# Two PSUM banks set aside for the rows that gathered expert rows are multiplied with

## The chip, the core and the metric

The kernel runs on one core of one Trainium2 chip. The metric is the device time of one execution in microseconds. TensorE appears as PE, VectorE as DVE, ScalarE as ACT, GpSimd as POOL and SyncE as SP.

## What is computed

One layer over 128 context tokens and 512 latent tokens, five blocks of 128 rows with 1024 columns. Each block goes through a modulated norm, a projection into two head groups (retention, and attention over a neighbourhood of the grid plus the context), an output projection, and a retrieval from 16384 single-neuron experts (PEER). The part that the change touches is the retrieval:

```python
def peer(x, wq, keys, u, v):
    q = (xb @ wq).reshape(TOKEN_BLOCK, PEER_HEADS, PEER_DKEY)
    s1 = jnp.einsum('nhd,hkd->nhk', q[..., :half], keys[:, 0])
    s2 = jnp.einsum('nhd,hkd->nhk', q[..., half:], keys[:, 1])
    v1, i1 = lax.top_k(s1, PEER_TOPK)
    v2, i2 = lax.top_k(s2, PEER_TOPK)
    ...
    eidx = jnp.take_along_axis(cidx, sel, axis=-1)
    gate = jax.nn.softmax(top, axis=-1)
    act = jax.nn.gelu(jnp.einsum('nd,nhkd->nhk', xb, u[eidx]))
    return jnp.einsum('nhk,nhkd->nd', gate * act, v[eidx])
```

For each row of a block, 8 heads choose 16 experts each. Its 128 rows of `u` are multiplied with the row itself (`xb`, called x2 in the kernel), and the products weight 128 rows of `v`.

## The kernel before

Block 0 holds the context tokens, blocks 1 to 4 the latent tokens. `ctx_front` takes block 0 up to its expert scores. `lat_front` does the same for the latent blocks: common projections, then block 1 (`ROUNDS[0]`), then blocks 2 to 4 (`ROUNDS[1]`). In `mix`, `attend` runs the neighbourhood attention one unit (a head of a block) after another, and `retain` the retention. `close` does the output projection, the second norm (`modulate2`, which makes x2) and the scores (`key_scores`).

`gathers` runs beside this. For each of the five blocks it does 128 steps of kind "u": an indirect DMA from POOL's queue brings 128 rows of `u` (512 KB) into a slot of `gslots`, and one DVE instruction multiplies them with x2 and sums along the row. The slot is then free for another gather. Before each block a step of kind "x2" brings the block's x2. The top-16 searches (`topk`) are DVE work as well. At the end come 128 steps of kind "v" for block 4, which DVE sums up in PSUM.

For blocks 0 to 3 the sum over `v` is a dense product. `Dense.build` turns a block's choices and weights into a 128 x 128 x 128 table W, by one-hot matrices (two DVE comparisons with `iota2`, two ACT scalings and two small matmuls per pair of rows). `product` then streams all of `v` through PE, first for blocks 0 and 1, then for blocks 2 and 3. The builds for blocks 2 and 3 overwrite the tables of blocks 0 and 1 behind the first product. The second product needs the last build.

PSUM has eight banks of 512 columns. `bank()` takes one between two bounds, which `within` sets for a piece of work. `attend` had banks 0 to 3, and `retain`, `project` and `close` banks 4 to 7 while they ran beside it. One unit of attention takes two banks for its scores and two for its transposes, beside the bank `bo` that collects the outputs of a pair of heads.

The program is not emitted as written. Every call is recorded in `Plan`, which finds what each instruction depends on (memory cells, one cell for each bank) and orders them all by a list scheduler with costs of its own. `keep` (L365 in every row is the line that issues) hides the source lines, so rows are told apart by tiles and shapes: `psum<-arena,w 128x128` and `128x384` are key_scores with a weight tile, `128x256` with `iota` is a build, `dots` is a gather's multiply.

The places that the prediction speaks of:

```python
    gslots = [zone[1]] + zone[6:]
    ...
                b2, b = bank(), bank()
                mm(b2.ap[:, :P], lq, kctx.ap[q, p, :], True, True)
                mm(b.ap, lq, nkT.ap[q, p, :], True, True)
    ...
                nc.vector.scalar_tensor_tensor(g, g, 1.0, x2p[0], op0=OP.mult, op1=OP.mult,
                                               accum_out=dots[b % 2][:, h, k:k + 1])
```

Four more slots join `gslots` when `lat_front` has used its inputs, and one when `close` has ended; block 3's x2 goes to PSUM (banks 6 and 7) and so gives its slot back.

Of the kernel before, what the change touches and what calls it, by code (L numbers as in the profile page):

```python
# [17 lines left out]
OP = mybir.AluOpType  # L18
AX = mybir.AxisListType

D = 1024
P = 128
# [346 lines left out]
def layer(ctx: ExitStack, tc: tile.TileContext, a: dict):  # L369
# [31 lines left out]
    ar.limit = (TOT - ZONE) // UNIT  # L401
    ar.soft = 48 * 256 // UNIT
    zone = [shaped(ar.tile[:, TOT - ZONE:], [SLOTS, D])[:, i] for i in range(SLOTS)]
    gslots = [zone[1]] + zone[6:]
    ps = Mem(pp.tile([P, 8 * 512], F32, name="psum"), 8 * 512, 512)
    xres = hb.tile([5, P, D], F32, name="xres")
    xmod = hb.tile([5, P, D], F32, name="xmod")
# [5 lines left out]
    def bank():  # L413
        return ps.alloc([512], lo=banks[0], hi=banks[1])
# [498 lines left out]
    def key_scores(key, bl, x2T):  # L913
        T = P * len(bl)
        for m4 in range(4):
            bs = [bank() for _ in range(4)]
            for qt in range(4):
                w = S.get(("wq", key, m4, qt))
                for m in range(4):
                    for e in range(2):  # L920
                        c = 2 * qt + e
                        mm(bs[m].ap[:, :T], w[:, e, P * m:P * m + P], x2T[:, c, :], c == 0, c == 7)
                S.done()
            q = ar.alloc([4, T])
            for m, b in enumerate(bs):
                nc.scalar.copy(q.ap[:, m], b.ap[:, :T])
                ps.free(b)
            for i, blk in enumerate(bl):
                b = bank()
                for m in range(4):  # L930
                    mm(b.ap[:, P * m:P * m + P], q.ap[:, m, P * i:P * i + P], keysT.ap[:, 4 * m4 + m, :], True, True)
                if blk == 2:
                    t = half()
                    nc.scalar.copy(t, b.ap.rearrange("q (m k) -> q m k", m=4))
                    ps.free(b)
                    ready[blk, m4] = t
                    yield
                    continue
                t = ar.alloc([4, P], top=blk < 1)
                nc.scalar.copy(t.ap, b.ap.rearrange("q (m k) -> q m k", m=4))  # L940
                ps.free(b)
                if blk < 2:
                    ready[blk, m4] = t
                else:
                    nc.sync.dma_start(scd[blk, m4], t.ap.rearrange("q m k -> q (m k)"))
                    ar.free(t)
                    ready[blk, m4] = "dram"
                yield
            ar.free(q)


    def ctx_front():
# [114 lines left out]
        make_gates(0, ("g1", "sh2", "a2"))  # L1067
        yield from out_proj(0, 0, [oN.ap], [oR.ap], [xc.ap])
        ar.free(oR, oN)
        x2T = ar.alloc([8, P])  # L1070
        yield from modulate2(0, 0, xc.ap, zone[0], x2T.ap, 0)
        ar.free(xc)
        ar.free(*[gates.pop((n, 0)) for n in ("g1", "sh2", "a2")])
        yield from key_scores(0, [0], x2T.ap)
        ar.free(x2T)
# [9 lines left out]
    def lat_front():  # L1085
# [183 lines left out]
        def each(bl, fn, out):  # L1269
            for i in bl:  # L1270
                out[i] = yield from fn(i)
                yield
# [27 lines left out]
            yield from transposed(r, rqT)  # L1300

        def mix(bl):
            return both(within(4, 8, each(bl, retain, oR)), within(0, 4, attend(bl)))

        def close(key, bl, last):
            xs = []
# [19 lines left out]
            else:  # L1326
# [2 lines left out]

        S.quota = NRING - 2  # L1330
        yield from project(1, ROUNDS[0])
        yield from both(within(4, 8, project(2, ROUNDS[1])),
                        within(0, 4, chain(each(ROUNDS[0], retain, oR), attend(ROUNDS[0]))))
        make_gates(1, ("g1", "sh2", "a2"))
        make_gates(1, ("g2",))
        ar.free(mrow, selr, selc, scs)
        ar.free(hT, ct)
        lend(XTRA)
        yield from both(within(4, 8, close(1, ROUNDS[0], False)), mix(ROUNDS[1]))
        close_lent()  # L1340
        ar.free(nkT, kctx, vctx, Sst, *o[6].values())
        yield from close(2, ROUNDS[1], True)
# [90 lines left out]
    STEPS = 36  # L1433

    cready = {}
    x2p, x2b = [zone[0]], []

    def gathers():
        seq = []
# [36 lines left out]
        while n < len(seq):  # L1476
# [7 lines left out]
            n += 1  # L1484
            if kind == "u":
                h, k = divmod(s, 16)
                nc.vector.scalar_tensor_tensor(g, g, 1.0, x2p[0], op0=OP.mult, op1=OP.mult,
                                               accum_out=dots[b % 2][:, h, k:k + 1])
                hp, q = divmod(s, 32)
                nxt = (b, hp + 1) if hp < 3 else (b + 1, 0)  # L1490
# [17 lines left out]
                    nc.vector.tensor_mul(c, c, z1)  # L1508
                    cready[b, hp - 1] = cready[b, hp] = True
            elif kind == "x2":  # L1510
                if "lat" not in done:
                    x2p[0], g = g, x2p[0]
                else:
                    if b == 3:
                        gslots.append(x2p[0])
                        x2b.append(ps.alloc([D], lo=6))
                        x2p[0] = x2b[0].ap
                    for hf in range(2):
                        nc.scalar.copy(x2p[0][:, 512 * hf:512 * hf + 512], g[:, 512 * hf:512 * hf + 512])
            elif kind == "v":  # L1520
                h, k = divmod(s, 16)
                if s == 0:
                    ps.free(*x2b)
                    accv = ps.alloc([D], lo=6)
                    nc.vector.tensor_scalar(accv.ap, g, cw[b][:, h, k:k + 1], None, op0=OP.mult)
                else:
                    nc.vector.scalar_tensor_tensor(accv.ap, g, cw[b][:, h, k:k + 1], accv.ap, op0=OP.mult, op1=OP.add)
            elif kind == "g2":
                held = g
            else:  # L1530
                finish_with(4, [accv.ap[:, 0:512], accv.ap[:, 512:]], held, g)
                mark.append(len(nc.ops) - 7)
                done.add("v4")
# [279 lines left out]
```

## Time and profile before

| | |
|---|---|
| device time, median of 3 runs | 1914.18 us (1909.31 to 1915.98) |
| device time of the profiled execution | 1914.02 us |
| span of the profiled execution | 1912.2 us |
| PE, DVE, ACT, POOL busy | 94%, 77%, 28%, 43% of the span |
| mean granted TensorE clock | 0.947 |
| moved by DMA | 658.22 MB, mean 344 GB/s |

The span is what the trace covers; the device time is 1.8 us longer. A busy PE is not one at its peak: at a granted clock of 0.5 the same matmul takes twice as long.

### The profile page before, as it was taken

Reading aid. Unit: us, or ns where it says so; the run is one execution under the profiler, and the core shown is the slowest. Engines: PE = TensorE matmul, PEld = TensorE weight load, DVE = VectorE, ACT = ScalarE, POOL = GpSimd, SP = SyncE. Lnnn points to the kernel's source line nnn. Section 1 sums busy time; section 2 is a strip of 40 time slices with the busy share of each in tenths; the row PEclk is TensorE's granted clock in tenths of the full one; section 3 lists DMA queues with packets and bytes.
Section 4 is the critical chain, followed back from the end, with each engine's and each line's share of the span. In section 5 each row is a group of like instructions: output and inputs, shape, how many; then the busy total and the mean of one; then the engine's idle time right before and its main releaser. Section 6 shows DMA issues by size and latency. Waiting matters only on the chain.

```text
span 1912.2 us, 21190 instructions
## 1 busy us (share of the span) xinstructions
PE 1798.2 (94%) x6096; PEld 1074.3 (56%) x6096; DVE 1468.8 (77%) x3785; ACT 532.4 (28%) x1368; POOL 825.7 (43%) x779
## 2 busy tenths in 40 slices
PE   7989999999989979977999999899997999999997
PEld 2438454455955546656544444455565666666665
DVE  2245998777787799999999998778999565666666
ACT  1225321134433424699311110123574000000000
POOL 0000556543145456533555554444535444444442
PEclk9998999999968889976899999999997999999999
DMA  9997879988768799966899999999988999999998
GB/s 363 314 330 245 305 275 335 385 317 321 265 199 288 264 325 383 376 180 196 317 409 409 407 403 409 386 408 403 386 266 285 409 409 409 409 410 409 409 409 342
DMA packets 203693, 658.22 MB, mean 344 GB/s; under 512 B 22572, under 2 KB 25900, under 8 KB 203448
## 3 DMA queue, kind: packets, MB, share of 16 engines
q0 software_dynamic: 110592, 402.70, 56.7%
q1 hardware_dynamic: 92984, 254.16, 35.2%
q8 instruction: 49, 0.80, 0.2%
q14 instruction: 68, 0.56, 0.1%
HBM read 645.51 MB, written 11.27 MB: 343 GB/s over the span
## 4 chain that ended last, share of the span: by engine, by line
PE 46%; DMA 32%; DVE 16%; issue 4%; ACT 2%; POOL 0%; DVEq 0%; SPq 0%; POOLq 0%; ACTq 0%
PE psum L365 46%; DMA arena<-in_u,idx 15%; DMA arena<-in_v,idx 12%; DVE arena L365 11%; ACT arena L365 2%; DMA w<-in_w_ada 2%; DVE psum L365 1%; DMA w<-in_w_in 1%; DVE i L365 1%; DVE oh L365 1%; DVE vi L365 1%; DMA arena<-in_x 1%; DMA arena<-in_w_ada 0%; DMA arena<-in_selc 0%; DMA g2d<-arena 0%
## 5 line engine op out<-in xcount | busy, mean ns | idle before, releaser
L365 PE MATMUL psum<-w,arena 128*128 128x512 f32 (+1 forms) x2548 | 1099.5, 603 | 17.1 <-DVE arena L365 6.5
L365 POOL DMA_INDIRECT arena<-in_u,idx x640 | 702.5, 1098 | 918.0 <-DVE arena L365 482.7
L365 PEld LDWEIGHTS psum<-w,arena 128*128 128x128 f32 (+1 forms) x2548 | 561.5, 229 | 459.1 <-issue 288.6
L365 PE MATMUL psum<-arena 128*128 128x128 f32 (+5 forms) x2532 | 551.1, 370 | 57.6 <-DVE arena L365 29.4
L365 PEld LDWEIGHTS psum<-arena 128*128 128x128 f32 (+2 forms) x2532 | 378.2, 208 | 270.1 <-issue 152.5
L365 DVE SCALAR_TENSOR_TENSOR arena<-arena 128x1024 f32<-128x1024 f32 (+6 forms) x451 | 489.2, 1092 | 33.2 <-DMA arena<-in_u,idx 27.7
L365 DVE SCALAR_TENSOR_TENSOR arena<-arena,psum 128x1024 f32<-128x1024 f32 x256 | 308.6, 1215 | 88.2 <-DMA arena<-in_u,idx 87.9
L365 ACT ACTIVATE arena<-arena 128x128 f32<-128x128 bf16 (+7 forms) x626 | 237.8, 433 | 223.8 <-PE psum L365 108.0
L365 ACT COPY arena<-psum 128x512 f32<-128x512 f32 (+3 forms) x360 | 204.7, 580 | 331.9 <-PE psum L365 301.2
L365 DVE SCALAR_TENSOR_TENSOR psum<-arena,cw,psum 128x1024 f32<-128x1024 f32 x127 | 163.7, 1289 | 94.8 <-DMA arena<-in_v,idx 94.5
L365 DVE TENSOR_TENSOR arena<-iota,arena 128x256 bf16<-128x256 bf16 (+1 forms) x512 | 162.1, 355 | 32.1 <-PE psum L365 26.9
L365 POOL DMA_INDIRECT arena<-in_v,idx x128 | 120.2, 939 | 143.6 <-DVE psum L365 118.7
L365 PE MATMUL psum<-arena,w 128*128 128x128 f32 (+1 forms) x640 | 135.5, 371 | 1.4 <-ACT arena L365 1.4
L365 PEld LDWEIGHTS psum<-arena,w 128*128 128x128 f32 x640 | 95.4, 202 | 31.6 <-ACT arena L365 2.2
L365 PE MATMUL psum<-ident,arena 128*128 128x128 f32 x372 | 70.0, 317 | 27.7 <-DVE arena L365 25.0
L365 PEld LDWEIGHTS psum<-ident,arena 128*128 128x128 f32 x372 | 52.0, 165 | 65.7 <-DVE arena L365 29.0
L365 DVE TENSOR_TENSOR arena<-arena 128x256 f32<-128x256 f32 (+6 forms) x131 | 61.6, 500 | 10.0 <-ACT arena L365 3.2
L365 ACT ACTIVATE zz<-dots 128x64 f32<-128x64 f32 x10 | 2.6, 261 | 189.9 <-DVE arena L365 189.7
L365 DVE TENSOR_TENSOR arena<-psum,arena 128x512 f32<-128x512 f32 (+1 forms) x40 | 26.9, 686 | 35.2 <-PE psum L365 32.9
L365 DVE TENSOR_REDUCE arena<-arena 128x8 f32<-128x512 f32 (+1 forms) x17 | 12.7, 744 | 46.6 <-ACT arena L365 46.6
L365 ACT ACTIVATE arena<-psum,arena 128x128 f32<-128x128 f32 (+2 forms) x102 | 34.7, 431 | 33.8 <-PE psum L365 29.6
L365 DVE MAX8 vi<-arena 128x8 f32<-128x128 f32 x128 | 30.3, 280 | 14.5 <-ACT arena L365 14.5
(74 smaller groups left out, 502.2 us busy)
## 6 DMA issues: line engine op xcount, KB each, us to landing
w<-in_v SPq DMA_DIRECT2D x251, 512.0 KB, 6.8
w<-in_w_ada SPq DMA_DIRECT2D x41, 512.0 KB, 5.8
w<-in_wq SPq DMA_DIRECT2D x40, 512.0 KB, 6.2
w<-in_w_in SPq DMA_DIRECT2D x36, 512.0 KB, 11.0
arena<-in_u,idx POOLq DMA_INDIRECT x640, 8.6
arena<-in_w_in SPq DMA_DIRECT2D x16, 512.0 KB, 10.7
w<-in_w_out SPq DMA_DIRECT2D x16, 512.0 KB, 6.0
arena<-in_x SPq DMA_DIRECT2D x9, 512.0 KB, 8.9
```

The source lines that it names most:

```text
L365: getattr(getattr(self.nc, eng), fn)(*args, **kw)
```

## The change

The two banks 6 and 7 hold x2 for all blocks, from block 0 on. All other work after `ctx_front`'s norm lives in banks 0 to 5. `attend` has three banks in place of four, and the work beside it three. `key_scores` makes its four products in two passes of two banks, and holds four weight tiles at a time. The slot that held x2 (`zone[0]`) is a gather slot from the start; where x2 of blocks 1 and 2 was taken over by swapping slots, it is now copied into PSUM by two ACT instructions, as for block 3 and 4 before.

```diff
-    gslots = [zone[1]] + zone[6:]
+    gslots = zone[:2] + zone[6:]
...
     def key_scores(key, bl, x2T):
         T = P * len(bl)
         for m4 in range(4):
-            bs = [bank() for _ in range(4)]
-            for qt in range(4):
-                w = S.get(("wq", key, m4, qt))
-                for m in range(4):
-                    for e in range(2):
-                        c = 2 * qt + e
-                        mm(bs[m].ap[:, :T], w[:, e, P * m:P * m + P], x2T[:, c, :], c == 0, c == 7)
-                S.done()
             q = ar.alloc([4, T])
-            for m, b in enumerate(bs):
-                nc.scalar.copy(q.ap[:, m], b.ap[:, :T])
-                ps.free(b)
+            ws = [S.get(("wq", key, m4, qt)) for qt in range(4)]
+            for m in range(0, 4, 2):
+                bs = [bank() for _ in range(2)]
+                for c in range(8):
+                    for e, b in enumerate(bs):
+                        mm(b.ap[:, :T], ws[c // 2][:, c % 2, P * (m + e):P * (m + e) + P], x2T[:, c, :], c == 0, c == 7)
+                    if m and c % 2:
+                        S.done()
+                for e, b in enumerate(bs):
+                    nc.scalar.copy(q.ap[:, m + e], b.ap[:, :T])
+                    ps.free(b)
...
-        yield from modulate2(0, 0, xc.ap, zone[0], x2T.ap, 0)
-        ar.free(xc)
+        yield from modulate2(0, 0, xc.ap, x2.ap, x2T.ap, 0)
+        banks[:] = [0, 6]
+        x2p.append(ps.alloc([D], lo=6))
+        for hf in range(2):
+            nc.scalar.copy(x2p[0].ap[:, 512 * hf:512 * hf + 512], x2.ap[:, 512 * hf:512 * hf + 512])
+        ar.free(xc, x2)
...
-            return both(within(4, 8, each(bl, retain, oR)), within(0, 4, attend(bl)))
+            return both(within(3, 6, each(bl, retain, oR)), within(0, 3, attend(bl)))
...
-        yield from both(within(4, 8, close(1, ROUNDS[0], False)), mix(ROUNDS[1]))
+        yield from both(within(3, 6, close(1, ROUNDS[0], False)), mix(ROUNDS[1]))
...
             elif kind == "x2":
-                if "lat" not in done:
-                    x2p[0], g = g, x2p[0]
-                else:
-                    if b == 3:
-                        gslots.append(x2p[0])
-                        x2b.append(ps.alloc([D], lo=6))
-                        x2p[0] = x2b[0].ap
-                    for hf in range(2):
-                        nc.scalar.copy(x2p[0][:, 512 * hf:512 * hf + 512], g[:, 512 * hf:512 * hf + 512])
+                for hf in range(2):
+                    nc.scalar.copy(x2p[0].ap[:, 512 * hf:512 * hf + 512], g[:, 512 * hf:512 * hf + 512])
```

Since the scheduler plans the whole program again, instructions stand in another order on every engine.

PE, late in the attention of blocks 2 to 4, before the change. `128x128` from the arena is a unit's product with the context keys, `128x512` with the latent keys, `128x64` its values, `ident` its five transposes, `w` a tile of other weights.

```order
L365 MATMUL psum<-w_92,arena 128x512
L365 MATMUL psum<-arena 128x512
L365 MATMUL psum<-arena 128x64 x5
L365 MATMUL psum<-ident,arena 128x128 x5
L365 MATMUL psum<-arena 128x128
L365 MATMUL psum<-arena 128x512
```

The same place after the change:

```order
L365 MATMUL psum<-arena 128x128
L365 MATMUL psum<-ident,arena 128x128 x4
L365 MATMUL psum<-arena 128x512
L365 MATMUL psum<-ident,arena 128x128
L365 MATMUL psum<-arena 128x64 x5
```

A unit's two score products stood together, and the five transposes too. Now four transposes stand between the two score products, and the fifth behind them: each pair takes turns in the same two banks.

DVE, at the end of the last build, before the change. `iota` rows are the build's comparisons, `dots` rows the gathers' multiplies; the last row is what follows the build.

```order
L365 TENSOR_TENSOR arena<-iota_65,arena 128x256 x3
L365 SCALAR_TENSOR_TENSOR arena,dots_77<-arena,psum 128x1024
L365 TENSOR_TENSOR arena<-iota_65,arena 128x256
L365 SCALAR_TENSOR_TENSOR arena,dots_77<-arena,psum 128x1024
L365 TENSOR_TENSOR arena<-iota_65,arena 128x256 x2
L365 SCALAR_TENSOR_TENSOR arena,dots_77<-arena,psum 128x1024
L365 TENSOR_TENSOR arena<-iota_65,arena 128x256
L365 SCALAR_TENSOR_TENSOR arena,dots_77<-arena,psum 128x1024 x22
```

After the change:

```order
L365 TENSOR_TENSOR arena<-iota_65,arena 128x256 x4
L365 SCALAR_TENSOR_TENSOR arena,dots_77<-arena,psum 128x1024
L365 TENSOR_TENSOR arena<-iota_65,arena 128x256 x4
L365 SCALAR_TENSOR_TENSOR arena,dots_77<-arena,psum 128x1024
L365 TENSOR_TENSOR arena<-iota_65,arena 128x256
L365 SCALAR_TENSOR_TENSOR arena,dots_77<-arena,psum 128x1024 x21
```

Before, a multiply stood after every two comparisons or so; now after every four. Counted in the whole order, 26 multiplies stood between the end of the first product's matmuls and the last comparison, and 21 do now; in the builds that come ahead of the first product (from the last 128x384 matmul of key_scores on) 40 stood among 192 comparisons, and 47 among 198 do now. At the first comparison of the first build 214 multiplies were behind, and 227 are now; at the last comparison of the second, 300 and 309; at the last of all, 554 and 556 of 767.

## Rows read from the trace of the kernel before

**Rows 1.** the page: busy us; then tenths in 40 slices of the span.

```profile
PE 1798.2 (94%) x6096; PEld 1074.3 (56%) x6096; DVE 1468.8 (77%) x3785; ACT 532.4 (28%) x1368; POOL 825.7 (43%) x779
...
PE   7989999999989979977999999899997999999997
```

**Rows 2.** five stages: busy us and instructions by engine, clock, DMA.

```profile
560.00:694.00 134.00, 116.86 (x473) 67.29 (x471) 105.02 (x291) 48.87 (x139) 65.01 (x56) 0.86 0.83 281
...
796.00:921.00 125.00, 99.10 (x459) 80.83 (x458) 119.22 (x349) 115.46 (x274) 45.24 (x46) 0.74 0.70 216
921.00:1408.00 487.00, 478.48 (x1359) 232.18 (x1358) 433.20 (x1293) 113.87 (x327) 249.49 (x236) 0.99 1.01 395
1408.00:1470.00 62.00, 45.99 (x224) 36.43 (x222) 60.40 (x160) 45.28 (x126) 25.08 (x26) 0.82 0.76 239
1470.00:1902.00 432.00, 431.81 (x1000) 295.47 (x1000) 270.27 (x309) 2.52 (x9) 193.05 (x206) 0.99 1.02 406
```

**Rows 3.** timeline at the end: start, us, engine, operation, count, idle before.

```profile
1894.50 7.46 PE L365 MATMUL psum<-w,arena 128*128 128x512 f32 x17
...
1900.63 1.29 DVE L365 SCALAR_TENSOR_TENSOR psum<-arena,cw,psum 128x1024 f32<-128x1024 f32 x1 [1.25 <-DMA arena<-in_v,idx]
...
1904.35 1.29 DVE L365 TENSOR_TENSOR psum<-psum,w 128x512 f32<-128x512 f32 x2
```

**Rows 4.** groups by form: busy us, mean ns of one, idle time before them.

```profile
L365 DVE SCALAR_TENSOR_TENSOR arena<-arena 128x1024 f32<-128x1024 f32 x389 | 471.9, 1216 | 28.4 <-DMA arena<-in_u,idx 27.7
...
L365 DVE SCALAR_TENSOR_TENSOR arena<-arena,psum 128x1024 f32<-128x1024 f32 x256 | 308.6, 1215 | 88.2 <-DMA arena<-in_u,idx 87.9
...
L365 ACT COPY psum<-arena 128x512 f32<-128x512 f32 x4 | 2.3, 582 | 3.5 <-DMA arena<-xmod 3.5
```

**Rows 5.** gather issues on POOL from 200 to 1080 us, by form.

```profile
L365 POOL DMA_INDIRECT arena<-in_u,idx x371 | 437.7, 1180 | 448.1 <-DVE arena L365 247.8 <-DVE idx L365 59.5 <-issue 46.3
```

**Rows 6.** the same from 1100 to 1625 us.

```profile
L365 POOL DMA_INDIRECT arena<-in_u,idx x256 | 249.7, 976 | 279.6 <-DVE arena L365 233.4 <-DVE i L365 11.6 <-issue 7.0
```

**Rows 7.** timeline, PE, in key_scores of the context block.

```profile
166.20 1.06 PE L365 MATMUL psum<-arena 128*128 128x128 f32 x8
...
167.09 7.31 PE L365 MATMUL psum<-arena,w 128*128 128x128 f32 x64
```

**Rows 8.** the page, DMA issues: KB each, median us from issue to landing.

```profile
w<-in_wq SPq DMA_DIRECT2D x40, 512.0 KB, 6.2
```

**Rows 9.** timeline of the attention on blocks 2 to 4.

```profile
622.63 0.74 DVE L365 CUSTOM_DVE_ANT_0 arena<-psum,w,arena 128x512 f32<-128x512 f32 x1
...
622.98 0.71 PE L365 MATMUL psum<-ident,arena 128*128 128x128 f32 x5
...
623.48 1.22 DVE L365 SCALAR_TENSOR_TENSOR arena<-arena 128x1024 f32<-128x1024 f32 x1
...
623.63 2.60 PE L365 MATMUL psum<-arena 64*128 64x512 f32 x14
623.74 0.59 ACT L365 COPY arena<-psum 128x512 f32<-128x512 f32 x1 [0.17 <-PE psum L365]
...
626.07 0.71 PE L365 MATMUL psum<-ident,arena 128*128 128x128 f32 x5
```

**Rows 10.** timeline, DVE passes over latent scores, first and last of 18.

```profile
565.51 0.75 DVE L365 CUSTOM_DVE_ANT_0 arena<-psum,w,arena 128x512 f32<-128x512 f32 x1
...
657.62 0.75 DVE L365 CUSTOM_DVE_ANT_0 arena<-psum,w,arena 128x512 f32<-128x512 f32 x1
```

**Rows 11.** timeline of DVE in the last build.

```profile
1435.38 1.15 DVE L365 TENSOR_TENSOR arena<-iota,arena 128x256 bf16<-128x256 bf16 x4
1436.46 1.21 DVE L365 SCALAR_TENSOR_TENSOR arena<-arena,psum 128x1024 f32<-128x1024 f32 x1
...
1437.60 1.15 DVE L365 TENSOR_TENSOR arena<-iota,arena 128x256 bf16<-128x256 bf16 x4
```

More of the change, by code (lines that the diff above doesn't have):

```diff
@@ L1069, in ctx_front @@
         ar.free(oR, oN)
-        x2T = ar.alloc([8, P])
-        yield from modulate2(0, 0, xc.ap, zone[0], x2T.ap, 0)
-        ar.free(xc)
+        x2T, x2 = ar.alloc([8, P]), ar.alloc([D])
+        yield from modulate2(0, 0, xc.ap, x2.ap, x2T.ap, 0)
[4 more added lines that the diff above has]
+        ar.free(xc, x2)
         ar.free(*[gates.pop((n, 0)) for n in ("g1", "sh2", "a2")])
@@ L1331, in lat_front @@
         yield from project(1, ROUNDS[0])
-        yield from both(within(4, 8, project(2, ROUNDS[1])),
-                        within(0, 4, chain(each(ROUNDS[0], retain, oR), attend(ROUNDS[0]))))
+        yield from both(within(3, 6, project(2, ROUNDS[1])),
+                        within(0, 3, chain(each(ROUNDS[0], retain, oR), attend(ROUNDS[0]))))
         make_gates(1, ("g1", "sh2", "a2"))
@@ L1435, in layer @@
     cready = {}
-    x2p, x2b = [zone[0]], []
+    x2p = []
     def gathers():
@@ L1486, in gathers @@
                 h, k = divmod(s, 16)
-                nc.vector.scalar_tensor_tensor(g, g, 1.0, x2p[0], op0=OP.mult, op1=OP.mult,
+                nc.vector.scalar_tensor_tensor(g, g, 1.0, x2p[0].ap, op0=OP.mult, op1=OP.mult,
                                                accum_out=dots[b % 2][:, h, k:k + 1])
@@ L1522, in gathers @@
                 if s == 0:
-                    ps.free(*x2b)
+                    ps.free(x2p[0])
                     accv = ps.alloc([D], lo=6)
```

## The prediction

> **What bounds the kernel now.** I read the page first, then the end of the timeline, then the busy times by stage. PE is busy for 94% of the span, and the slices show where it isn't: it is full for most of the run, and short in slices 15, 18, 19 and 31 of 40 [rows 1]. The stages tell more [rows 2]. In the last one (1470 to 1902 us) and in 921 to 1408 us PE is busy throughout at a granted clock of 0.99, so these are the dense products at PE's own pace; DMA is full there too (406 and 395 GB/s), because the gathers take what the product's stream of `v` leaves. In between stand three stages in which PE waits or runs slow: the attention (560 to 694 us, clock 0.86), the first two builds (796 to 921 us, clock 0.74, DVE busy for 119.2 of 125 us and ACT for 115.5), and the last build (1408 to 1470 us, DVE busy for 60.4 of 62 us). There the end is set by DVE, ACT and the hand-overs between them.
>
> At the end two chains arrive together [rows 3]: the last dense matmul ends at 1894.50 + 7.46 = 1901.96 us, and the last multiply of the gathers at 1900.63 + 1.29 = 1901.92 us. So a gain for the gathers alone is worth nothing beyond the last few microseconds, and a loss on PE's way counts in full. Two questions decide: does PE get later with two banks fewer, and can the gathers, which get a slot more, give something back to PE's way?
>
> **The change part by part.** The sum is made against the profiled execution, 1914.0 us, which is 0.2 us from the median of the runs shown.
>
> *The multiply with x2 in PSUM: nothing.* Both forms are in the trace: 1216 ns with x2 in SBUF, 1215 ns with x2 in PSUM [rows 4]. 384 multiplies change from one to the other at no cost. The new copies into PSUM are two of 582 ns each for blocks 0, 1 and 2 [rows 4]; a block's first multiply waits 1.2 us for them. The gathers have that time, as they come out ahead below; without that cover the three would cost 3.5 us.
>
> *One slot more.* Up to some 900 us six slots turn, and then seven; from there DMA is full [rows 2], and a further slot gains nothing. Before, the seventh slot lets the order move multiplies forward: 13 more are behind at the first build, 9 more when the dense product starts, 2 more at the last build's end. In the last stage 206 gathers were issued in 432 us [rows 2], 2.10 us each, so the gathers' own end comes 2 x 2.10 = 4 us earlier against PE's. All that this saves is the finish of block 4 (1901.95 to 1904.35 us [rows 3]), which can then run before PE ends: **-2 us** (0 to -2.4).
>
> *Gather issue on POOL.* An issue took 1180 ns on average up to 1080 us, and 976 ns from 1100 us on, where x2 lay in PSUM [rows 5, 6]. That is 0.2 us less for 384 gathers, and POOL waits for longer than it issues in both stretches (448 of idle for 438 us of work), mostly for DVE to free a slot: off the path, nothing. The Trainium skill has a rule on this: the page "GPSIMD Engine Reference", section "Specifications", says that GpSimd shares its SBUF interfaces with VectorE and contends with instructions that have two SBUF inputs. The trace agrees with it (1180 against 976 ns). By the rule alone, with POOL as the bound, up to 384 x 0.2 = 77 us would go; by the rows of the end, where PE arrives at the same moment, none of it does.
>
> *key_scores in two passes.* The matmuls are the same in number. For the context block a step of 32 products took 7.31 us and its scores 1.06 us [rows 7]. Now four of the six weight tiles are held, and the first is free again only a quarter into the second pass: at 3.65 + 0.9 us. The same tile is wanted by the next step's third quarter of its first pass, some 2.7 + 1.06 + 1.8 = 5.6 us later, and a load takes 6.2 us at the median [rows 8]. So 0.6 us may be missing in each of three steps: **+1.5 us** (0 to 6, if loads take two microseconds longer). For blocks 2 to 4 the products are three times as long and hide the load; evictions have four banks to turn in.
>
> *Attention with three banks: the main term.* The fast units of before are 3.09 us apart (transposes at 622.98 and 626.07 us [rows 9]) with PE full. Now scores and transposes share two banks. From one latent score product to the next, each must wait for the other: the product (two records, together 2 x 431.81 / 1000 = 0.86 us by the last stage [rows 2]), DVE's pass over it 0.74, four transposes 0.55 (four fifths of 0.71), ACT's copy 0.59 [rows 9], and four hand-overs of about 0.2 (0.17 shown before the copy): 3.5 us. A gather's multiply often stands before DVE's pass; it holds DVE for 1.14 us, so half of that on average: 4.1 us. That is 1.0 us more for each fast unit. PE runs in order, so what stands behind the waiting transpose waits too: the values of the unit before, and the weight products put there as filler. But few units are so fast: 18 units have their DVE pass between 565.51 and 657.62 us [rows 10], so they are 92.1 / 17 = 5.4 us apart on average, because of filler and of stretches at the low clock (0.86 granted in the stage [rows 2]); there the chain fits. I count six fast units (+6 us) and four changes of a pair, where the output bank can't be swapped for a free one (+1 us each): **+10 us**. Bounds: 0 if filler always covers the wait, and 24 units x 1.0 = 24 us if it never does; with the clock down further from 0.86, by 0.04 of 134 us, 30 us. I take a value nearer to the lower end because most units are slow already.
>
> *The first two builds.* Here the extra multiplies land in a stage in which DVE is full. From the last key_scores product to the first dense one the order has 47 in place of 40, and 198 comparisons in place of 192, with 9 small top-16 instructions fewer (0.2 us each, an estimate from the rest of the stage). A multiply takes 1.14 us from start to start, four comparisons 1.08 us [rows 11]: 7 x 1.14 + 6 x 0.27 - 9 x 0.2 = 7.8 us. ACT, busy for 115.5 of 125 us, gets nearly nothing more, so if ACT sets the pace most of it is hidden: between 0 and 8, I take **+6 us**, by DVE's larger share.
>
> *The last build.* Five multiplies fewer (21 for 26), two comparisons and three small ones more: -5.7 + 0.5 + 0.4 = **-5 us** (0 to -6). PE has nothing else there but the second product, which needs the build.
>
> The sum: 1914.0 - 2 + 1.5 + 10 + 6 - 5 = 1924.5, so **1924 us**, 0.5% slower. What a run can tell from no change is about 0.3%, 5.7 us.
>
> **The rivals.**
> *The banks cost nothing (0.20).* The filler covers every wait, the rest stays: 1914.0 - 2 + 1.5 + 6 - 5 = 1914.5. For it: PE was fully busy in much of the attention, and the scheduler knows the banks. Against it: PE's order is fixed, and it waits wherever a real duration differs from the planned one. That the seventh slot does nothing belongs here, since gathers alone don't set the end.
>
> *Faster, by the builds (0.13).* The one mechanism is that multiplies are moved out of the last build into a stage where they are hidden: the first builds would be paced by ACT (115.5 of 125 us), and the 7 extra multiplies would fit into what DVE has left. Then 1914.0 - 2 + 1.5 + 0 - 5 = 1908.5 with the attention at zero, and 1904 where better spacing on DVE returns some of the clock in that stage (0.74). It decides if attention and first builds together cost less than about 1 us. Against it: DVE has only 6 us left in that stage.
>
> *Faster, by the gathers (0.05).* If PE arrives at the end with the gathers only because the gathers take DMA from its stream of `v`, then 9 gathers less behind the start of the dense product are worth 9 x 2.10 = 19 us, and the time is 1895. The quicker issue on POOL works in the same direction. Against it: PE is full in that stage, at a clock of 0.99, so it doesn't wait for `v` [rows 2]. The page "GPSIMD Engine Reference" of the Trainium skill speaks for this rival, by the contention named above.
>
> *Much slower (0.15).* The waits in the attention come at every unit and pull the clock down: 1914.0 - 2 + 6 + 30 + 8 - 5 = 1951; half way from the forecast, about 1938. For it: the clock was at 0.86 there already, with fewer waits.
>
> **How the numbers follow.** The forecast's case, between 1916 and 1934 us, has 0.47. The range must leave no more than 2 in 10 outside: it reaches down to 1904, over the two likelier rivals below, and up to 1944, the middle of the slow one. Chances: faster by over 0.3% (below 1908.3) 0.13 and 0.05 of the two faster rivals and 0.03 of the first, 0.21; within 0.3% 0.16 of the first and 0.02 of the forecast's lower edge, 0.18; slower 0.45 of the forecast, 0.15 of the last rival and 0.01 of the first, 0.61.
>
> **What would show it.** Right: between the attention's first and last DVE pass over scores the stretch is about 10 us longer, with PE waiting for ACT and DVE in front of transposes and products, and units some 4 us apart where they were 3.1; the builds ahead of the first product take about 131 us in place of 125; the last build takes 57 in place of 62; gather issues take about 1.0 us throughout; the last v multiply ends some microseconds ahead of the last matmul. Wrong: if the attention isn't longer, or if the clock in the builds and the attention moves by more than 0.04 either way, since that is worth as much as any term here.

## The result and the profile after

The changed kernel took 1929.68 us (median of 6 runs, 1925.69 to 1940.00), the kernel before 1915.31 beside it (6 runs, 1909.31 to 1920.07). The ratio is 1.008, with a 95% interval of 1.0056 to 1.0104: slower by 0.8%. The profiled execution took 1927.41 us, 13.4 more than that of before. Ratios here and below are of executions at most 1.5% longer than the fastest of the same kernel, which leaves out three of twelve in the run e4 and one of twelve in e10.

The milestones are the same instructions in both: the last product of the context's key_scores, the first and the last of the 18 DVE passes [rows 10] (of the 24 that blocks 2 to 4 have in all, the last 18), the first and last 128x384 matmul of the latent key_scores, the first dense product, the last build's last matmul, the last matmul. A row gives the start, the end and the length of a stage in us, then busy time and number of instructions of PE, PEld (PE's loading of weights), DVE, ACT and POOL, then PE's granted clock, and DMA's busy share and GB/s. Before:

```profile
182.20:565.50 383.30, 368.01 (x1469) 210.75 (x1468) 313.02 (x854) 111.70 (x277) 175.84 (x147) 0.96 0.85 305
565.50:657.60 92.10, 87.69 (x366) 51.20 (x366) 68.49 (x211) 37.50 (x106) 47.42 (x40) 0.83 0.79 262
657.60:698.10 40.50, 28.50 (x106) 17.18 (x106) 38.67 (x93) 12.45 (x35) 17.48 (x15) 0.86 0.94 338
698.10:800.80 102.70, 102.67 (x425) 67.74 (x424) 99.61 (x289) 44.75 (x108) 69.17 (x55) 0.99 0.97 364
800.80:914.40 113.60, 87.70 (x413) 72.93 (x411) 108.60 (x321) 106.43 (x253) 38.90 (x41) 0.73 0.68 208
914.40:1469.50 555.10, 531.07 (x1602) 273.04 (x1602) 499.19 (x1464) 163.09 (x461) 278.31 (x263) 0.97 0.98 376
1469.50:1902.00 432.50, 431.81 (x1000) 295.47 (x1000) 270.77 (x309) 3.01 (x9) 193.50 (x206) 0.99 1.02 406
1902.00:1909.20 7.20, 0.00 (x0) 0.00 (x0) 7.20 (x12) 0.00 (x0) 0.00 (x0) 0.71 0.40 149
```

The same stages after:

```profile
183.20:561.90 378.70, 367.66 (x1463) 209.86 (x1463) 310.04 (x853) 114.37 (x281) 140.63 (x146) 0.96 0.86 310
561.90:668.50 106.60, 94.87 (x358) 54.69 (x357) 84.17 (x241) 38.07 (x106) 48.59 (x51) 0.76 0.82 281
668.50:718.40 49.90, 41.10 (x122) 23.98 (x122) 42.38 (x116) 12.86 (x38) 16.41 (x18) 0.76 0.86 299
718.40:821.60 103.20, 101.03 (x413) 66.23 (x414) 98.82 (x333) 46.64 (x116) 45.76 (x47) 1.00 0.88 327
821.60:937.80 116.20, 88.25 (x424) 73.65 (x422) 112.18 (x312) 107.18 (x252) 44.54 (x47) 0.75 0.74 226
937.80:1486.10 548.30, 529.69 (x1602) 272.00 (x1602) 480.12 (x1381) 158.66 (x452) 245.11 (x253) 0.98 0.97 372
1486.10:1918.60 432.50, 431.86 (x1000) 295.41 (x1000) 271.01 (x310) 3.00 (x9) 191.63 (x204) 0.99 1.02 404
1918.60:1922.70 4.10, 0.01 (x1) 0.00 (x0) 4.06 (x7) 0.00 (x0) 0.00 (x0) 0.88 0.61 227
```

Stage by stage the difference is +1.0 up to the first bound, then -4.6, **+14.5**, **+9.4**, +0.5, +2.6, -6.8, 0 and -3.1: together 13.5, the measured 13.4. The attention and the output projection behind it lose 23.9 us; the other stages together give 10.4 back.

The waits of PE in the attention's stretch, before and then after (us in total, times, longest):

```profile
PE psum L365 <- ACT arena L365: 4.9, 8, 0.7
```

```profile
PE psum L365 <- ACT arena L365: 11.6, 21, 0.7
```

PE stood 4.4 us before and 11.7 after; the other half of the 14.5 is busy time, 87.7 against 94.9 us. It is about the same amount of work at a lower clock: busy time by clock is 72.8 before (87.69 x 0.83) and 72.1 after (94.87 x 0.76), an estimate. (The work is not quite the same: 14 products of the output projection have left the stretch, and 6 with weight tiles have come.)

Two units of the attention after, PE, in a stretch with the clock at 1.00:

```profile
624.09 1.12 PE L365 MATMUL psum<-arena 64*128 64x512 f32 x2 [0.67 <-ACT arena L365]
625.14 0.33 PE L365 MATMUL psum<-ident,arena 128*128 128x128 f32 x1
625.30 1.64 PE L365 MATMUL psum<-arena 128*128 128x64 f32 x12
626.88 0.66 PE L365 MATMUL psum<-ident,arena 128*128 128x128 f32 x4
628.21 1.12 PE L365 MATMUL psum<-arena 64*128 64x512 f32 x2 [0.67 <-ACT arena L365]
```

The latent product waits for ACT's copy of the four transposes, whose bank it takes. A unit comes every 4.12 us (628.21 - 624.09), where the fast ones of before were 3.09 us apart [rows 9]. DVE's pass over the scores and ACT's copy in the first of these units:

```profile
625.25 0.75 DVE L365 CUSTOM_DVE_ANT_0 arena<-psum,w,arena 128x512 f32<-128x512 f32 x1 [0.51 <-PE psum L365]
...
627.57 0.59 ACT L365 COPY arena<-psum 128x512 f32<-128x512 f32 x1 [1.74 <-PE psum L365]
```

The pass waits for PE and ends at 626.00 us; the next four transposes start at 626.88, right behind PE's values of the unit. So DVE does not hold PE up here: the 4.12 us are 3.45 of PE's own work and one wait of 0.67 for ACT's copy.

The groups behind the attention (657.6 to 698.1 us before, then 668.5 to 718.4 after):

```profile
L365 PE MATMUL psum<-arena 128*128 128x512 f32 x34 | 14.8, 592 | 0.0
L365 PE MATMUL psum<-ident,arena 128*128 128x128 f32 x38 | 8.6, 377 | 10.8 <-DVE arena L365 10.2 <-ACT arena L365 0.6
```

```profile
L365 PE MATMUL psum<-arena 128*128 128x512 f32 x48 | 22.0, 615 | 0.0
L365 PE MATMUL psum<-ident,arena 128*128 128x128 f32 x37 | 8.9, 396 | 7.2 <-DVE arena L365 6.6 <-ACT arena L365 0.6
```

More large products, 48 for 34, stand behind the last pass, and cost 7.2 us. The 14 stood between the attention's units before.

DVE in the first builds, then in the last build (1443.2 to 1486.1 us), after:

```profile
L365 DVE TENSOR_TENSOR arena<-iota,arena 128x256 bf16<-128x256 bf16 (+1 forms) x197 | 61.1, 360 | 4.0 <-PE psum L365 2.9 <-ACT arena L365 0.9
L365 DVE SCALAR_TENSOR_TENSOR arena<-arena,psum 128x1024 f32<-128x1024 f32 x47 | 56.8, 1208 | 0.0
```

```profile
L365 DVE SCALAR_TENSOR_TENSOR arena<-arena,psum 128x1024 f32<-128x1024 f32 x17 | 20.4, 1210 | 0.0
```

POOL's gather issues after, from 200 to 1080 us, and the end of PE and of DVE's gathers:

```profile
L365 POOL DMA_INDIRECT arena<-in_u,idx x371 | 359.0, 968 | 526.7 <-DVE arena L365 311.1 <-DVE idx L365 58.8 <-DVE cand L365 52.8
```

```profile
1894.41 24.20 PE L365 MATMUL psum<-w,arena 128*128 128x512 f32 x56
...
1913.84 1.29 DVE L365 SCALAR_TENSOR_TENSOR psum<-arena,cw,psum 128x1024 f32<-128x1024 f32 x1 [1.23 <-DMA arena<-in_v,idx]
```

An issue takes 968 ns where it took 1180 [rows 5]. The last gather's multiply ends at 1915.13, 3.5 us ahead of the last matmul (1918.61).

### The profile page after: what moved, and what is told of

Its sections match the earlier page's. It is cut to its first block, busy times and chain, and to the rows that moved or that the text cites. A ratio compares the mean times of both kernels' runs of the same rounds, so it can differ in the third digit from the quotient of the medians.

```text
span 1925.6 us, 21225 instructions
## 1 busy us (share of the span) xinstructions
PE 1813.5 (94%) x6096; PEld 1080.0 (56%) x6096; DVE 1466.3 (76%) x3785; ACT 534.2 (28%) x1374; POOL 738.6 (38%) x779
## 4 chain that ended last, share of the span: by engine, by line
PE 48%; DMA 28%; DVE 15%; issue 5%; ACT 3%; POOL 1%; DVEq 0%; SPq 0%; POOLq 0%; ACTq 0%
PE psum L365 48%; DMA arena<-in_v,idx 12%; DMA arena<-in_u,idx 11%; DVE arena L365 10%; ACT arena L365 2%; POOL arena L365 1%; DVE psum L365 1%; DMA w<-in_w_in 1%; DMA w<-in_bias 1%; DMA w<-in_wq 1%; DMA w<-in_w_ada 1%; DVE i L365 1%; DVE oh L365 1%; DVE vi L365 1%; DMA arena<-in_w_ada 0%
## 5 line engine op out<-in xcount | busy, mean ns | idle before, releaser
L365 POOL DMA_INDIRECT arena<-in_u,idx x640 | 615.4, 962 | 1017.7 <-DVE arena L365 576.0
L365 DVE SCALAR_TENSOR_TENSOR arena<-arena,psum 128x1024 f32<-128x1024 f32 x640 | 770.6, 1212 | 105.1 <-DMA arena<-in_u,idx 104.0
L365 PE MATMUL psum<-arena 128*128 128x128 f32 (+5 forms) x2532 | 563.3, 375 | 61.1 <-DVE arena L365 35.3
L365 PEld LDWEIGHTS psum<-arena 128*128 128x128 f32 (+2 forms) x2532 | 385.3, 211 | 272.8 <-issue 150.4
L365 PE MATMUL psum<-ident,arena 128*128 128x128 f32 x372 | 74.1, 321 | 20.0 <-DVE arena L365 16.7
L365 DVE DVE_READ_ACCUMULATOR arena<-arena,psum 128x1 f32 x640 | 52.0, 81 | 0.0
```

Source lines behind the costliest of these rows:

```text
L365: getattr(getattr(self.nc, eng), fn)(*args, **kw)
```

## The experiments

The theory: with three banks PE waits more often in the attention, and the granted clock falls with these waits. The rivals: the seventh slot (51 multiplies stand in the stretch for 41 before, though e1 and e2, with six slots, have 49); and the new plan itself, whatever it was made for. "Stretch" is the time from the first to the last of the 18 passes, "waits" PE's waits for ACT in it (times), "units" how far apart the passes come where they follow each other most evenly (for the kernel before, fastest). Stretch, clock, waits and units are of one profiled execution each. The kernel before took 1912.3 us beside the first four runs, 1925.8 beside the next four and 1927.7 beside the last four, each group on another chip, so times are compared as ratios to it, and a stage of such a profile can differ from that of before by some microseconds for this alone.

| run | attention's banks | ratio to before, 95% interval | stretch us | clock | waits us | units us |
|---|---|---|---|---|---|---|
| before | 4 | 1 | 92.1 | 0.83 | 4.9 (8) | 2.9 to 3.6 |
| the change | 3 | 1.008, 1.0056 to 1.0104 | 106.5 | 0.76 | 11.6 (21) | 3.7 to 4.3 |
| e1_banks_alone | 3 | 1.0296, 1.0268 to 1.0324 | 124.2 | 0.65 | 13.5 (21) | 6.6 to 6.9 |
| e2_six_slots | 3 | 1.0244, 1.0216 to 1.0272 | 120.1 | 0.66 | 12.5 (21) | 6.8 to 6.9 |
| e3_attend_three | 3 | 1.0145, 1.0118 to 1.0171 | 122.7 | 0.71 | 11.8 (19) | 6.9 to 7.0 |
| e4_psum_later | 4 | 1.0039, 1.0007 to 1.0070 | 100.8 | 0.65 | 4.6 (7) | 3.7 to 4.4 |
| e5_filler | 3 | 1.0109, 1.0068 to 1.0151 | 92.5 | 1.00 | 3.7 (7) | 3.9 to 4.2 |
| e6_replan_before | 4 | 1.0055, 1.0026 to 1.0085 | 91.5 | 0.83 | 3.1 (6) | 3.0 to 4.0 |
| e7_replan_after | 3 | 1.0113, 1.0068 to 1.0159 | 109.8 | 0.72 | 10.0 (18) | 4.1 |
| e8_replan_six | 3 | 1.0152, 1.0112 to 1.0192 | 115.4 | 0.68 | 10.2 (16) | 4.6 to 5.9 |
| e9_three_held | 3 | 1.0150, 1.0120 to 1.0179 | 107.2 | 0.79 | 10.3 (17) | 4.1 |
| e10_fill_three | 3 | 1.0091, 1.0055 to 1.0127 | 97.0 | 1.00 | 3.6 (7) | 4.2 |
| e11_fill_later | 3 | 1.0060, 1.0041 to 1.0079 | 97.2 | 0.95 | 5.2 (9) | 3.6 to 4.5 |
| e12_fill_replan | 3 | 1.0112, 1.0080 to 1.0144 | 100.0 | 0.97 | 6.7 (11) | 4.2 |

**Banks alone.** The kernel before with the bounds of the change, key_scores in two passes, and nothing for x2 or the slots:

```diff
+        banks[:] = [0, 6]
...
-            return both(within(4, 8, each(bl, retain, oR)), within(0, 4, attend(bl)))
+            return both(within(3, 6, each(bl, retain, oR)), within(0, 3, attend(bl)))
...
```

> The kernel before with the banks of the change alone: six banks in place of eight from the context block's scores on, three banks each for the attention and what runs beside it, key_scores in two passes. x2 stays in SBUF, six slots turn. Theory (the attention's third bank is what PE's way lost): the stretch from the first to the last of the 18 latent score passes (92.1 us before, 106.5 after) is 102 us or more, fast units come 3.7 to 4.3 us apart where they were 2.9 to 3.6, and the time is 1922 to 1936 us, at least what the change itself takes (1929.7), since the gains at the last build (-5) and the end (-3) belong to the slot. Rival (the seventh slot brings more multiplies in front of the score passes): the stretch is under 97 us, and the time 1911 to 1918. Rival (any new plan moves the stretches about by some 10 us): the attention may be anything, and stages that the banks do not touch differ by 5 us or more as well.

The loss, 3.0%, is over twice what the theory allowed at most (1936 us, 1.2%), and the units come 6.6 to 6.9 us apart, not 3.7 to 4.3. Of the 57.8 us between this profile and that of before 32.1 lie in the attention, 10.8 ahead of it, 9.5 in the output projection and 7.9 in the first builds, so the rival of the plan is not out by this run: other stages moved too. PE in this kernel's attention:

```profile
645.84 1.11 PE L365 MATMUL psum<-ident,arena 128*128 128x128 f32 x4
647.62 2.69 PE L365 MATMUL psum<-arena 64*128 64x512 f32 x4 [0.68 <-ACT arena L365]
650.10 0.42 PE L365 MATMUL psum<-ident,arena 128*128 128x128 f32 x1
650.32 2.53 PE L365 MATMUL psum<-arena 128*128 128x64 f32 x10
652.78 1.11 PE L365 MATMUL psum<-ident,arena 128*128 128x128 f32 x4
```

and its window:

```profile
645.80:659.70 13.90, 12.55 (x39) 8.05 (x38) 7.12 (x21) 4.32 (x10) 3.69 (x5) 0.50 0.67 196
```

It is the changed kernel's row of instructions with the same wait of 0.68 us, but at half clock (1.2 GHz): a unit takes 6.94 us (652.78 - 645.84), of which 6.26 are PE's own work, in place of 3.45. The rival of the slot falls: with six slots the stretch is longer, not shorter.

**Six slots.** The changed kernel without its seventh slot until block 3:

```diff
-    gslots = zone[:2] + zone[6:]
+    gslots = [zone[1]] + zone[6:]
...
+                if b == 3:
+                    gslots.append(zone[0])
```

> The changed kernel with the seventh gather slot taken away again until block 3, as before; x2 in PSUM and six banks stay. Theory of the banks: the attention's stretch stays at 102 us or more and the time within 1922 to 1936 us; the last build, which took 43.5 us in place of 48.7 with the seventh slot, goes back to about 48, so 1929 to 1935 is likeliest. Rival of the slot: stretch under 97 us, time 1911 to 1918. Gather issues on POOL take about 1.0 us in both theories, as x2 is read from PSUM.

The stretch says banks again. The time lies above the ranges of both theories: 1958.7 us, 29 above the change.

**Three banks for the attention alone**, all else as before (block 1's retention, which runs in the attention's banks, gets three too):

```diff
-            return both(within(4, 8, each(bl, retain, oR)), within(0, 4, attend(bl)))
+            return both(within(4, 8, each(bl, retain, oR)), within(0, 3, attend(bl)))
...
-                        within(0, 4, chain(each(ROUNDS[0], retain, oR), attend(ROUNDS[0]))))
+                        within(0, 3, chain(each(ROUNDS[0], retain, oR), attend(ROUNDS[0]))))
```

> The kernel before with one edit: the attention has banks 0 to 2 in place of 0 to 3 (bank 3 lies idle there); its partners keep four, key_scores, slots and x2 are as before. Theory of the banks: the attention alone carries the loss, so the stretch of the 18 passes is 100 us or more, fast units come 3.7 us or more apart, and the time is 1920 to 1934 us. If it is the six banks elsewhere (the partner's three, key_scores in two passes) the stretch stays below 97 us and the time at 1911 to 1918 us. Rival of the slot: 1911 to 1918 too.

The stretch grows by 30.6 us and the time by 1.45%, to 1941 us, more than the 1934 that the theory allowed: the attention's bank does it without any other part of the change.

**x2 in PSUM after the attention.** The attention keeps four banks; x2 and the slot change over at block 2:

```diff
+        done.add("att")
+        banks[:] = [0, 6]
         yield from close(2, ROUNDS[1], True)
...
-                if "lat" not in done:
+                if "att" not in done:
...
-                    if b == 3:
+                    if not x2b:
```

> The kernel before with x2 moved into PSUM and the seventh slot given back at block 2 in place of block 3, that is after the attention, which keeps its four banks of eight; from there on six banks as in the change. Theory of the banks: the attention's stretch is as before (88 to 96 us), what the slot gives at the last build and the end remains (some -5 to -8), so 1904 to 1914 us, at least 10 us less than the change. Rival of the slot: as the slot comes after the attention, the same 1906 to 1914; it tells the two apart only together with the other runs. Rival of the new plan: 1905 to 1930, with no pattern.

The expectation failed: the stretch takes 100.8 us, not 88 to 96, and the median is 1926 us, not 1904 to 1914. Its runs go from 1907 us (mean clock 0.953) to 1940 us (0.939), and its profiled one (1934) is among the long ones. In it the stretch's clock is 0.65, as low as with the banks alone, but with four banks and only 4.6 us of waits. For 30 us PE does not stand at all, and the clock is at 0.50 all the same:

```profile
601.00:631.00 30.00, 30.00 (x99) 21.24 (x99) 18.11 (x51) 8.46 (x20) 10.41 (x11) 0.50 0.62 182
```

So waits of PE are not all that goes with a low clock, and what let it fall here is not settled. The stretch is 23 us shorter than that of e1 at the same clock, but it also holds fewer PE instructions (336 for 358), so how much of the 23 us the missing bank costs is not shown.

**Idle products.** The banks alone, in the same plan, with one product into an unread bank behind each unit's four transposes:

```diff
...
             getattr(getattr(self.nc, eng), fn)(*args, **kw)
+            if i in self.extra:
+                self.nc.tensor.matmul(**self.extra[i])
...
+                nc.extra[len(nc.ops) - 1] = dict(out=ps.tile[:, 7 * 512:], lhsT=t.ap[:, :P], rhs=t.ap[:, :512], start=True, stop=True)
```

> The kernel of the run with the banks alone (1970.7 us), its plan unchanged, with one idle product more per unit of the latent attention: behind the four transposes, where PE waits 0.68 us for ACT's copy, a 128x512 product of the unit's probabilities into a bank that nobody reads (32 in all, 0.43 us each at full clock, 0.86 at half). Theory of the clock: PE's small waits at three banks let the clock fall to half, and at half clock the same chain of hand-overs takes 6.9 us a unit in place of 4.1; with PE kept busy the clock stays up or comes back, so units come 4.0 to 5.0 us apart for most of the stretch, its granted clock is 0.80 or more (0.65 without), the stretch of the 18 passes falls from 124 to 95 to 112 us, and the time to 1935 to 1960 us although PE does more. Rival (the hand-overs themselves take the time, the clock only follows): units stay at 6.9 us or more, the stretch grows by up to 24 x 0.43 = 10 us, and the time is 1970 to 1985.

The stretch falls from 124.2 to 92.5 us and the ratio from 1.0296 to 1.0109, with more work on PE. The stretch is even shorter than the 95 to 112 us expected; the median, 1944 us, is in its range. (A product took 0.95 us, not 0.43.) PE in it, L367 being the idle product, and the stretch:

```profile
631.28 0.66 PE L365 MATMUL psum<-ident,arena 128*128 128x128 f32 x4
631.77 1.02 PE L367 MATMUL psum<-arena 128*128 128x512 f32 x2
632.73 1.12 PE L365 MATMUL psum<-arena 64*128 64x512 f32 x2
633.78 0.33 PE L365 MATMUL psum<-ident,arena 128*128 128x128 f32 x1
633.95 1.64 PE L365 MATMUL psum<-arena 128*128 128x64 f32 x12
635.52 0.66 PE L365 MATMUL psum<-ident,arena 128*128 128x128 f32 x4
```

```profile
571.70:664.20 92.50, 87.64 (x392) 48.40 (x392) 82.32 (x231) 37.67 (x102) 62.66 (x48) 1.00 0.89 316
```

The wait is filled, PE never stands here, the clock stays at 1.00 (2.4 GHz), and a unit takes 4.24 us. That is no quicker than in the changed kernel, since PE is now busy for the whole unit; but it is far from the 6.94 at half clock. But for these products every engine has the same instructions in the same order in both traces, so the order of the plan is no rival here.

**New plans.** One constant of the planner's cost for DVE (`66` to `70`), in the kernel before, in the changed one, and in the one with six slots.

> The kernel before with nothing changed but one constant by which the planner costs VectorE's instructions (70 cycles in place of 66), so that its order comes out different at many places. Theory of the banks: resources set the time, 1906 to 1920 us, the attention's stretch 85 to 100 us. Rival (any new plan moves the time): 1925 or more, with the attention's clock under 0.75, since it would show that an order alone costs what the banks are blamed for.

> The changed kernel with the same constant changed. If the seven slots and x2 in PSUM are what gives back most of the 57 us that the banks alone cost, the time stays at 1923 to 1938 us. If the changed kernel's plan was a lucky one, it goes towards the runs with three banks in the attention: 1940 to 1970 us, with units 6.9 us apart at half the clock.

> The changed kernel with the seventh slot taken away, and the same constant changed. If the slot is worth some 29 us (1958.7 against 1929.7), this is 1950 to 1967 us and 15 us or more above the changed kernel with the same constant. If the two differed by the luck of their plans, the two come out within 10 us of each other, or the other way round.

A new plan alone costs the kernel before 0.55%. On the scale of the first four runs that is 1923 us, just above the expected 1906 to 1920; the rival, which wanted 1925 us or more with the attention's clock under 0.75, is not met either, as the attention is unchanged (91.5 us, 0.83). Between this profile and that of before lie 26.6 us, and the largest part, 13.4, lies between the first dense product and the last build (568.5 us for 555.1). There PE waits 8.70 us for DVE at a place that took 6.06 before, and 4.48 for a row of `v`, together 7.1 us more:

```profile
1245.50 0.47 PE L365 MATMUL psum<-ident,arena 128*128 128x128 f32 x1 [8.70 <-DVE arena L365]
...
1476.06 2.08 PE L365 MATMUL psum<-w,arena 128*128 128x512 f32 x2 [4.48 <-DMA w<-in_v]
```

The kernel before itself took some 10 us more beside these runs than in its profile's group, so not all of this is the plan's.

In the changed kernel the constant leaves the attention with 18 waits and 109.8 us, and its units stay 4.1 us apart, not 6.9; the ratio, 1.0113, can't be told from the change's 1.008. So nothing here says that the changed kernel's plan was a lucky one. The slot's 29 us do not come back: 1.0152 without it and 1.0113 with it overlap, and the medians lie 4.6 us apart, as expected if the two had differed by their plans.

**Idle products elsewhere.** A control with four banks everywhere but in the attention, bank 3 held free there (`spare.append(ps.alloc([512], lo=3, hi=4))`); the same plan with the idle products into bank 3 (these overwrite something there that another stage still needs, so the second output is another one; the instructions are the same); the banks alone with the products and with x2 in PSUM and the seventh slot from block 2 on (the two edits of e4 and e5); and e5 with the constant at 70.

> The kernel before with banks 0 to 2 for the attention, and bank 3 reserved and never written there; the rest has its banks as before. It is the control of the next run, with the same plan. Theory of the clock: as the earlier run with three banks in the attention (1.0145 times the kernel before): ratio 1.008 to 1.020, the stretch of the 18 passes 105 to 125 us at a granted clock of 0.65 to 0.78. If three banks with this plan keep the clock by luck, ratio 0.998 to 1.006, and the next run can show little.

> The run before this one in the same plan, with one idle 128x512 product per unit into bank 3 behind the four transposes (32 in all). Theory of the clock: the stretch of the 18 passes takes 85 to 98 us at a granted clock of 0.90 or more, the time is 10 to 30 us under its control, at 0.988 to 1.004 of the kernel before: three banks for the attention then cost nothing, and four are not what the attention needs. Rival (waits for banks by themselves): the time is that of the control or up to 14 us more.

> Six banks for all other work as in the change, with key_scores in two passes; x2 in SBUF and six slots during the attention; the idle products in bank 7 during the attention; after it x2 in banks 6 and 7 and the seventh slot from block 2 on. Theory of the clock: the attention's stretch is 88 to 98 us at a clock of 0.90 or more, and the time 0.996 to 1.008 of the kernel before, less than the run with banks alone and the same products (1.0109), since x2 in PSUM and the slot come earlier. Rival (the slot and x2 in PSUM gave back nothing by themselves): 1.008 to 1.016.

> The run with the banks alone and the idle products, planned with VectorE's constant changed (70 in place of 66). If what a new plan does to the time goes by the clock in the attention, then with the clock kept two plans come out alike: the stretch of the 18 passes within 6 us of 92.5, at a clock of 0.92 or more, and the ratio to the kernel before within 0.006 of 1.0109. If plans differ otherwise too, the ratio is off by more, with the difference in other stages.

In all four the attention does nearly as expected: 107.2 us without the products, 97.0 to 100.0 with them at a clock of 0.95 or more. Two bounds are missed narrowly: e9's clock is 0.79 where at most 0.78 was expected, and e12's stretch 100.0 us where it was 98.5 (PE also waits 4.4 us for DVE there). The times follow only in part: those of e9, e11 and e12 lie in their ranges, but against its control e10 gains only 0.6%, at the edge of the intervals, and misses its ratio of at most 1.004. Its runs go from 1932 us (mean clock 0.972) to 1961 us (0.944). The profiled executions of e5, e10 and e12 are each the shortest of their kernel, so the high clock in the stretch is shown for these and not for every execution. No kernel here beats the one before.

## Why the prediction was right, and where it was off

**The forecast** (1924 us, 0.5% slower) had the sign and nearly the size: 0.8%. But the sum came out through terms that it did not have, and that it came so near is in part luck: the attention and the output projection cost 13.9 us more than forecast, and 10.7 of that were offset by stages that did better than forecast (-4.6 ahead of the attention, -3.4 in the first builds, -1.6 in the products, -1.1 at the end).

**Attention with three banks, +10: +14.5. Right that PE waits, too small by the clock.** PE's waits for ACT rose by 6.7 us. What the term lacked is the clock: I put it at 0.86 and only let a further fall by 0.04 stand as the upper bound. It fell from 0.83 to 0.76, and busy time rose by the other 7.2 us. By the prediction's own words the clock would make it wrong if it moved by more than 0.04; it moved by 0.07 and by 0.10 behind the attention. That the floor of 4.1 us a unit met the trace's 4.12 is luck: it was added up from the product, DVE's pass with half a multiply ahead of it, the transposes, ACT's copy and the hand-overs, but in the units shown DVE's pass is not on this path. The rival "much slower" named the fall of the clock, and e1 to e3 show it at full size, 28 to 32 us. The idle products show that the clock is the lever: same plan, same banks, more work, 31.7 us less. The Trainium skill describes such a case: its page "TensorE: Matmul & The Clock Gate", section "A second HAM failure mode: psum-queue depth-cycling", tells of a kernel that cycles through PSUM banks and whose PE pauses often and briefly between groups of matmuls, so that the clock goes to and fro. The trace agrees (21 pauses of at most 0.7 us, clock 0.76), and e1 goes further: there the clock stays at 0.50 for whole runs of units. That nothing but the waits pulls the clock down is not shown: e4 has it at 0.65 with four banks and seven waits.

**Output projection behind the attention, +9.4: not in the sum.** I had counted only what lies between the first and the last pass. The products that had been filler between units stand behind them now, 14 records more (7.2 us), at 0.76. The attention's third bank by itself does not do this: with three banks in the attention alone, e3 keeps 24 of these products in the stretch and e9 14, while e4, with four banks, keeps none. So a plan can do it without a bank missing in the attention; whether it was the banks of the other work that did it in the changed kernel, no run here tells.

**First two builds, +6: measured +2.6.** The counts were right: 47 multiplies, and 197 records of the 198 comparisons. They brought 8.3 us more of multiplies (48.5 before) and 1.9 of comparisons (59.2), but DVE's whole busy time rose by only 3.6 us (108.6 to 112.2), since more of the top-16 work had left the stage than the 9 instructions at 0.2 us that I took off.

**Last build, -5: -5.2.** From 48.1 us (1421.4 to 1469.5) to 42.9, with 17 multiplies for 22 in that stretch.

**End, -2: -3.1; key_scores of the context, +1.5: +1.8** (34.1 to 35.9 us from its first to its last product, with three waits of 0.5 to 1.4 us for a weight tile). **Multiply and copies, 0:** 1212 ns for the multiply on average, and the copies 582 ns, as before.

**Gather issue, 0: right.** Issues fell to 968 ns, and POOL stood for 527 us in place of 448 [rows 5]. The Trainium skill's rule (page "GPSIMD Engine Reference", section "Specifications") holds: e1, with x2 in SBUF, has 1159 ns, e2, with x2 in PSUM, 964. It gave PE's way nothing that these runs show.

**The rivals on the other side** fell: banks that cost nothing, by e3; gains in the builds, by 116.2 for 113.6 us; the 19 us of the gathers, since PE's last stage took the same 432.5 us.

**What stays open.** The 0.8% is not far above the 0.55% that another plan costs by itself, so what the change moved in the other stages (-4.6 ahead of the attention, -1.6 in the products) can't be put down to the banks or to the slot. The attention's part can: without idle products all seven kernels with three banks have 16 to 21 waits and 106 to 124 us, the three with four banks 6 to 8 waits and 91 to 101. Why the banks alone stay 1.1% slower with the clock kept in the attention (e5, e12) isn't settled: in e5's profile the first builds take 127.6 us in place of 113.6, at a clock of 0.62 for 0.73, and the stage ahead of the attention 390.2 in place of 383.3. Neither is whether x2 in PSUM and the slot give back 0.5% there (e11), as its interval overlaps that of e5.

## What to carry to other kernels

Before taking a PSUM bank from a loop in which PE, ACT and DVE hand tiles over, count the hand-overs of one turn and then price the turn twice, at both levels of PE's clock: here the waits were 6.7 us of the 14.5. In a kernel whose order a planner makes, first time another order of the same instructions, since a change must beat what that moves. And look behind the stage that is changed: work that had filled its gaps is done there.

## Not expected of the hardware

The same instructions with the same wait run in two steady rhythms: 4.12 us a unit at a granted clock of 1.00 and 6.94 us at 0.50, for 16 us in the changed kernel and for 27 us with the banks alone, with PE busy for some 84% and 90% of that time. In e4 the clock stayed at 0.50 for 30 us in which PE never stood. And 32 products without use made a kernel faster: 1.0296 to 1.0109 of the kernel before.
